# Splitting the weights of k ahead, in the first FFN, and keeping them in DRAM

## The chip, the cores and the metric

The kernel runs on one core of one Trainium2 chip. The metric is the device time of one execution in microseconds (us); the number given for a kernel is the median over runs. The profile is of one further execution. Engines: TensorE (PE; PEld is its weight load), VectorE (DVE), ScalarE (ACT), GpSimd (POOL) and SyncE (SP), which only issues transfers here. "PEq", "SPq" and so on are the engines' queues.

## The reference

A decoder trunk of two layers on `x` of 512 tokens by 1024 channels, all in float32: a gated linear recurrence (LRU) and a feed-forward network (FFN), then a time mixing (RWKV-7) and a second FFN, each behind an RMS norm and added to `x`; one more RMS norm at the end. What matters here is the first FFN and the first projections of the mixing:

```
# FFN, twice: 1024 -> 2 x 3072 -> 1024
u    = rmsnorm(x) @ w_up
gate = causal_conv3(u[:, :3072]) + conv_b
x    = x + (gelu(gate) * u[:, 3072:]) @ w_down
# time mixing
h    = rmsnorm(x);  xx = shift(h) - h
r, k, v = ((h + xx * mix[i]) @ w_rkv[i] for i in (0, 1, 2))
w, a, g = small two-step projections of h + xx * mix[3], mix[4], mix[5]
... per head: scan over the tokens with r, k, v, w, a; group norm; times g; @ w_out
```

## The kernel before

**Matmuls in three passes.** TensorE multiplies in a 32-bit format that rounds (`F32R`). To keep float32 accuracy each operand is split in two parts, hi = round(x) and lo = round(x - hi), and each product is made of three matmuls, hi.hi, hi.lo and lo.hi (`mm3`). Activations stand as channels by tokens, 128 x 512.

**Weights.** `plan_weights` lists all weights in the order of their use as pieces of 512 KB (128 partitions x 1024 numbers). For each piece, `weights_load` gets a raw tile and a transfer on SyncE's queue (line 166); `weights_split` (line 172) makes hi by a copy on ScalarE (line 94) and lo by a subtraction on VectorE (line 97). `next_weights` (line 188) hands out the next piece; it loads three pieces ahead and splits two ahead. Raw, hi and lo tiles, as many other tiles, come from one set of 21 slots of 4 KB per partition, `b4`; a transfer or an operation that wants a slot waits until one is released. The matmuls of one piece are 24 of 512 columns.

**The first FFN.** The 3072 hidden channels are done as 12 pairs of blocks of 128. Pairs 0, 1, 2, 4, 6, 8 and 10 are "whole": four pieces G0, U0, G1, U1 (gate and up, each for half of the 1024 input channels). Pairs 3, 5, 7, 9 and 11 are "halves": they save a part of the matmuls by combining weight halves, partly with accumulating transfers on GpSimd's queue (lines 168 and 748), in products 1, 5, 6, 2, 7, 4, 3. After a halves pair comes a part of the down projection, whose first piece's matmuls stand before its products 4 and 3. One round, a whole pair, a halves pair and four pieces of down, takes 64 us. The gate's evacuation writes a padded tile `gpad`, the convolution and GELU make `ge` from it (`gate`, line 682), and the up part is multiplied by `ge`. Pair n uses `gpads[n % 2]`; `ge` has two buffers.

**The stage behind it.** The last down projection makes `x` block by block, and with it the next norm's squares. `rwkv_lora` multiplies the small projections, `rwkv_lora_k` starts k (its eight pieces in two groups of four; `project(mk, ...)`) together with the second step of the small projections; the second group of k stands at the start of `rwkv_krv`, beside `prepare`, which turns k, w and a into the scan's operands. Then come r (eight pieces), v, and the scan by chunks. The norm's root is computed on GpSimd (line 334), as are some constant tiles at the start of `rwkv_krv` (lines 1133 to 1141).

**Order.** A scheduler orders the instructions of each engine before the run, by their order in the program and its own estimate of when each can start; at run time every engine works through its queue in that order. Work at the side is written as generators in three lanes; `background(n, lane)` advances a lane by n steps, fractions adding up.

Of the kernel before, what the change touches and what calls it, by code (L numbers as in the profile page):

```python
# [7 lines left out]
F32 = mybir.dt.float32  # L8
F32R = mybir.dt.float32r
# [4 lines left out]
DRAM = bass.MemoryType.DRAM  # L14
NOSYNC = mybir.DependencyInfo(mybir.DependencyClass.NoSync, mybir.DependencyReason.DATA)

P = 128
D = 1024
T = 512
# [8 lines left out]
N4 = 21  # L28
WARM2 = 20
WARM = 14  # L30

HALVES = (3, 5, 7, 9, 11)

# [11 lines left out]
class Kernel:  # L45
# [54 lines left out]
    def plan_weights(self):  # L100
        I = self.I
        plan = []
        self.quads = []

        def piece(w, r0, c0, k):
            return w[r0 : r0 + k * P, c0 : c0 + D // k].rearrange("(k p) c -> p k c", p=P)

        def add(w, r0, c0, k=2):
            plan.append((piece(w, r0, c0, k), k, False, None))

        def full(w, groups, rows=8):
            for g in groups:
                for k in range(0, rows, 2):
                    add(w, k * P, g * 512)

        def ffn(l):
            up, dn = I["ffn_w_up"][l], I["ffn_w_down"][l]

            def gu(six):


                for n in range(2 * six, 2 * six + 2):
                    self.quads.append(len(plan))
                    a = lambda i, j: piece(up, j * 512, (1 - i) * DFF + n * 256, 4)
                    if n in HALVES:
                        for first, more in (((0, 0), None), ((1, 1), (1, 0)), ((0, 1), None), ((1, 0), (0, 0)), ((1, 1), None)):
                            plan.append((a(*first), 4, True, more and a(*more)))
                    else:
                        for i, j in ((1, 0), (0, 0), (1, 1), (0, 1)):
                            plan.append((a(i, j), 4, False, None))  # L130
                self.quads.append(len(plan))

            def dd(row, n):
                for g in range(2):
                    for k in range(0, n, 2):
                        add(dn, row + k * P, g * 512)

            gu(0)
            for six in range(1, 6):
                gu(six)  # L140
                if six < 5:
                    dd((six - 1) * 512, 4)
            dd(2048, 8)

        full(I["lru_w_in"][0], [2, 3, 0, 1])
        full(I["lru_w_out"][0], [0, 1])
        ffn(0)
        for i in (1, 0):
            full(I["rwkv_w_rkv"][0, i], [0, 1])
        for g in range(4):  # L150
            for k in range(0, 8, 4):
                add(I["rwkv_w_rkv"][0, 2], k * P, g * 256, 4)
        for h in range(2):
            for g in range(4):
                add(I["rwkv_w_out"][0], h * 512, g * 256, 4)
        ffn(1)
        self.plan = plan
        self.loaded, self.splitted = {}, {}
        self.n_load = self.n_split = self.n_used = 0

    def weights_load(self, upto):
        while self.n_load < min(upto, len(self.plan)):
            i = self.n_load
            src, k, _, more = self.plan[i]
            raw = self.b4(F32, (k, D // k), f"raw{i}")
            self.nc.sync.dma_start(raw, src)
            if more is not None:
                self.nc.gpsimd.dma_start(raw, more, accum_op=ALU.add)  # L168
            self.loaded[i] = raw
            self.n_load += 1  # L170

    def weights_split(self, upto, pin=False):
        while self.n_split < min(upto, len(self.plan)):
            i = self.n_split
            if self.plan[i][2]:
                self.n_split += 1
                continue
            self.weights_load(i + 1)
            raw = self.loaded.pop(i)
            k = self.plan[i][1]  # L180
            hi = self.b4(F32R, (k, D // k), f"wh{i}")
            lo = self.b4(F32R, (k, D // k), f"wl{i}")
            for j in range(k) if i == 0 else [slice(0, k)]:
                self.split(raw[:, j], hi[:, j], lo[:, j], pin=pin)
            self.splitted[i] = (hi, lo)
            self.n_split += 1
# [46 lines left out]
    def setup(self):  # L233
        self.tasks, self.due, self.done = ([], [], []), [0, 0, 0], set()
        nc, tc, ctx = self.nc, self.tc, self.ctx
        self.const = ctx.enter_context(tc.tile_pool(name="const", bufs=1))
        self.psum = ctx.enter_context(tc.tile_pool(name="psum", bufs=1, space=PSUM))
        self.xsp = ctx.enter_context(tc.tile_pool(name="xsp", bufs=1))
        dram = ctx.enter_context(tc.tile_pool(name="dram", bufs=1, space=DRAM))
        self.xd = dram.tile([P, KB, T], F32, name="xd")  # L240
        self.tgd = dram.tile([160, T], F32, name="tgd")
        c = self.const
        self.x = c.tile([P, KB, T], F32, tag="x", name="x", bufs=1)
        self.ident = c.tile([P, P], F32, name="ident")
        make_identity(nc, self.ident)
        self.inv_d = c.tile([P, 1], F32, name="inv_d")
        nc.vector.memset(self.inv_d, 1.0 / D)
        self.mhalf = c.tile([P, 1], F32, name="mhalf")
        nc.scalar.mul(self.mhalf, self.inv_d, -0.5 * D)
        self.pv = c.tile([P, 4 * P], F32, name="pv")  # L250
        self.col = {}
        for g, group in enumerate(PARAMS):
            r = 0
            for name, n in group:
                self.col[name] = g * P + r
                r += n
# [329 lines left out]
    def ffn(self, l, xs, finish, after=None):  # L586
        nc, tc = self.nc, self.tc
        last = l == 1
        with tc.tile_pool(name=f"ffn{l}", bufs=1) as pool:
# [1 line left out]
                return pool.tile([P, n], dt, tag=tag, name=tag, bufs=bufs)  # L591

            rbs, norm = [], []
            gpads = [pool.tile([P, 2, T + 2], F32, name=f"gpad{i}") for i in range(2)]
            for u in gpads:
                nc.vector.memset(u[:, :, 0:2], 0.0)
            late = []
# [78 lines left out]
            class Pair:  # L676

                def __init__(pair, n):
                    pair.n, pair.gp = n, gpads[n % 2]
                    pair.w, pair.bank, pair.s = {}, {}, {}  # L680

                def gate(pair, e):
                    if not e:
                        pair.ge = pool.tile([P, 2, T], F32, tag="ge", name="ge", bufs=2)
                    fb = 2 * pair.n + e
                    cv = t("cv", 2)
                    cw = lambda j: self.vec(f"ffn_conv_w{l}", j * FB + fb)
                    nc.scalar.activation(cv, pair.gp[:, e, 0:T], AF.Identity, bias=self.vec(f"ffn_conv_b{l}", fb), scale=cw(0))  # L688
                    for j in range(1, 3):
                        nc.vector.scalar_tensor_tensor(cv, pair.gp[:, e, j : j + T], cw(j), cv, ALU.mult, ALU.add)  # L690
                    nc.scalar.activation(pair.ge[:, e], cv, AF.Gelu_apprx_tanh)
# [5 lines left out]
            class Whole(Pair):  # L697
# [5 lines left out]
                def product(pair, p):  # L703
                    hi, lo = self.next_weights()
                    k0 = int(p[1]) * 4
                    for e in range(2):
                        if not k0:
                            pair.bank[p[0], e] = self.bank("acc" + p[0])
                        ps = pair.bank[p[0], e]
                        for k in range(4):  # L710
                            c = slice(e * P, e * P + P)
                            self.mm3(ps, (hi[:, k, c], lo[:, k, c]), xs[k0 + k][:2], k0 + k == 0, k0 + k == 7)
                        if p == "G1":
                            tt(pair.gp[:, e, 2:], ps, rbs[0], ALU.mult)
                            pair.gate(e)
                        if p == "U1":
                            if not e:
                                pair.room()
                            un = t("s", 7)
                            tt(un, ps, pair.ge[:, e] if last else rbs[0], ALU.mult)  # L720
                            if not last:
                                tt(un, un, pair.ge[:, e], ALU.mult)
                            self.split(un, pair.hid[:, e, 0], pair.hid[:, e, 1])
                        self.background(1)

            class Halves(Pair):

# [149 lines left out]

            for n in range(3, 12, 2):
                products((n, 7))
                if n == 11 and not last:  # L880
                    self.norm_begin()
                    self.push(self.lora_weights())
                down(n, 2 * n - 6, 4 if n < 11 else 8, lambda: products((n, 3)), lambda: ahead(at[0] + 2))
# [897 lines left out]
```

## Time and profile before

| | |
|---|---|
| median of 3 runs | 1290.84 us (1290.55 to 1292.97) |
| profiled execution | 1291.05 us, of it 1289.3 from the first to the last instruction (the span) |
| TensorE busy | 1264.2 us (98%) |
| VectorE busy | 928.1 us (72%) |
| ScalarE busy | 642.8 us (50%) |
| GpSimd busy | 133.6 us (10%) |
| moved by DMA | 141.37 MB, mean 110 GB/s |

Busy times are the engines' own; matmuls are pipelined, so a busy TensorE is not one at its peak. [...] "Idle before ... <- releaser" in a row is the time in which an engine stood still before that instruction, and what it waited for last.

### The profile page before, as it was taken

What the parts mean: (1) busy time and instruction counts of PE and PEld (TensorE: products, weight loads), DVE (VectorE), ACT (ScalarE), POOL (GpSimd) and SP (SyncE); (2) the same over time, 40 slices, a digit from 0 to 9 for tenths busy, and PEclk for the clock granted to TensorE, in tenths of its full rate; (3) what the DMA queues carried; (4) which work ended last, traced back from release to release, by engine and by line L of the source; (5) the groups of instructions that cost most, each with busy time, mean ns of one, the idle gap of its engine ahead of it and who ended that gap; (6) DMA issues with size and microseconds to landing.
All of it is one profiled execution on the core that took longest, in us unless ns stands there. A gap on an engine that the chain in (4) does not pass through costs nothing. (4 is left out here: it accounts for less than half of the span.)

```text
span 1289.3 us, 22401 instructions
## 1 busy us (share of the span) xinstructions
PE 1264.2 (98%) x9259; PEld 1067.0 (83%) x9259; DVE 928.1 (72%) x1412; ACT 642.8 (50%) x1006; POOL 133.6 (10%) x206
## 2 busy tenths in 40 slices
PE   9999999999999999999899999999999999999998
PEld 8777888989898888877678888778889898988886
DVE  5998678757575766788999967778766566666653
ACT  6797455434343443559844346545644334343432
POOL 3000001010101010010002145410010101010100
PEclk9999999999999999999999999999999999999999
DMA  7312335455454544422212122132344454545431
GB/s 222 111 55 94 98 122 108 150 112 159 103 164 98 170 95 116 144 79 82 79 41 87 52 62 84 44 99 82 116 96 161 101 170 92 178 84 179 100 131 65
DMA packets 117829, 141.37 MB, mean 110 GB/s; under 512 B 10138, under 2 KB 91748, under 8 KB 117600
## 3 DMA queue, kind: packets, MB, share of 16 engines
q1 hardware_dynamic: 100528, 122.44, 29.8%
q0 software_dynamic: 16624, 16.47, 8.4%
q8 instruction: 72, 1.18, 0.4%
q10 hardware_dynamic: 576, 1.05, 0.2%
q14 instruction: 29, 0.24, 0.1%
HBM read 135.41 MB, written 4.52 MB: 109 GB/s over the span
## 5 line engine op out<-in xcount | busy, mean ns | idle before, releaser
L97 DVE TENSOR_TENSOR wl<-raw,wh 128x1024 fp32r<-128x1024 f32 (+1 forms) x161 | 194.4, 1213 | 124.7 <-ACT wh L94 104.0
L94 ACT CAST wh<-raw 128x1024 fp32r<-128x1024 f32 (+1 forms) x161 | 165.9, 1043 | 195.2 <-PE acc L54 56.0
L54 PE MATMUL accG<-xs,wh 128*128 128x512 f32 x448 | 138.7, 391 | 0.0
L54 PE MATMUL accU<-xs,wh 128*128 128x512 f32 x448 | 138.6, 391 | 0.0
L54 PE MATMUL acc<-hid,wh 128*128 128x512 f32 x384 | 119.8, 395 | 0.0
L744 DVE TENSOR_TENSOR lo<-raw,hi 128x1024 fp32r<-128x1024 f32 x70 | 85.5, 1222 | 39.4 <-PE accU L54 32.0
L743 ACT CAST hi<-raw 128x1024 fp32r<-128x1024 f32 x70 | 73.6, 1052 | 60.7 <-PE accU L54 25.3
L54 PEld LDWEIGHTS accG<-xs,wh 128*128 128x128 f32 x448 | 83.7, 188 | 17.3
L54 PEld LDWEIGHTS accU<-xs,wh 128*128 128x128 f32 x448 | 83.7, 188 | 17.2
L54 PE MATMUL accG<-xs,wl 128*128 128x512 f32 x224 | 87.3, 390 | 0.0
L54 PE MATMUL accU<-xs,wl 128*128 128x512 f32 x224 | 87.3, 390 | 0.0
L54 PEld LDWEIGHTS acc<-hid,wh 128*128 128x128 f32 x384 | 71.3, 187 | 16.7
L54 PE MATMUL accA<-xt,hi 128*128 128x256 f32 x480 | 83.4, 277 | 0.0
L54 PE MATMUL acc<-xs,wh 128*128 128x512 f32 x256 | 81.1, 398 | 0.0
L690 DVE SCALAR_TENSOR_TENSOR cv<-gpad,pv,cv 128x512 f32<-128x512 f32 x96 | 69.1, 748 | 12.3 <-ACT cv L688 11.8
L845 PE MATMUL acc<-wl,hid 128*128 128x512 f32 (+1 forms) x200 | 77.2, 386 | 0.0
L844 PE MATMUL acc<-wh,hid 128*128 128x512 f32 (+1 forms) x200 | 77.0, 385 | 0.0
L843 PE MATMUL acc<-wh,hid 128*128 128x512 f32 (+1 forms) x200 | 76.7, 383 | 0.0
L168 POOL DMA_DIRECT2D raw<-in_ffn_w_up_dram x20 | 25.7, 1285 | 480.8 <-DMA raw<-in_ffn_w_up_dram 336.3
L54 PE MATMUL acc<-hid,wl 128*128 128x512 f32 x192 | 75.0, 395 | 0.0
L54 PEld LDWEIGHTS accA<-xt,hi 128*128 128x128 f32 x480 | 73.2, 188 | 0.9
L54 PE MATMUL accA<-xt,lo 128*128 128x256 f32 x240 | 66.3, 276 | 0.0
(411 smaller groups left out, 2943.1 us busy)
## 6 DMA issues: line engine op xcount, KB each, us to landing
raw<-in_ffn_w_up_dram SPq DMA_DIRECT2D x106, 512.0 KB, 3.7
raw<-in_ffn_w_down_dram SPq DMA_DIRECT2D x48, 512.0 KB, 3.9
raw<-in_ffn_w_up_dram POOLq DMA_DIRECT2D x30, 512.0 KB, 5.9
raw<-in_rwkv_w_rkv_dram SPq DMA_DIRECT2D x24, 512.0 KB, 3.7
raw<-in_lru_w_in_dram SPq DMA_DIRECT2D x16, 512.0 KB, 4.3
raw<-in_lru_w_out_dram SPq DMA_DIRECT2D x8, 512.0 KB, 3.7
raw<-in_rwkv_w_out_dram SPq DMA_DIRECT2D x8, 512.0 KB, 3.6
xd<-x SPq DMA_DIRECT2D x8, 256.0 KB, 2.0
```

The source lines that it names most:

```text
L54: mm = lambda *a, **kw: self.nc.tensor.matmul(ps, *a, skip_group_check=more, **kw)
L94: put = (self.nc.vector.tensor_copy if dve else self.nc.scalar.copy)(hi, src)
L97: self.nc.vector.tensor_tensor(lo, src, hi.bitcast(F32), ALU.subtract)
L168: self.nc.gpsimd.dma_start(raw, more, accum_op=ALU.add)
L690: nc.vector.scalar_tensor_tensor(cv, pair.gp[:, e, j : j + T], cw(j), cv, ALU.mult, ALU.add)
L743: nc.scalar.copy(hi, f[p])
L744: tt(lo, f[p], hi.bitcast(F32), ALU.subtract)
L843: nc.tensor.matmul(ps, hh[:, s], wh[:, k, m], start=kk == 0, stop=False)
L844: nc.tensor.matmul(ps, hl[:, s], wh[:, k, m], start=False, stop=False)
L845: nc.tensor.matmul(ps, hh[:, s], wl[:, k, m], start=False, stop=kk == blocks - 1)
```

## The change

The eight pieces of k's weights (`AHEAD = 8`) are split during the first FFN. A generator, `split_ahead`, is pushed to lane 1 after product 7 of pair 3. Each of its ten steps loads a raw piece on GpSimd's queue into a tile `early` of the FFN's pool (two buffers), stores the hi and lo parts of the piece split in the step before to DRAM, also on GpSimd's queue, and splits the piece loaded in the step before. Whole pairs advance it by 0.32 twice a product; what is left is done before the last down projection. When `weights_load` comes to one of these pieces it gets two `b4` tiles and fetches the stored hi and lo on GpSimd's queue; `weights_split` passes them through. The first FFN now has one `gpad` and one `ge` buffer in place of two each (the second FFN keeps two).

```diff
@@ -29,6 +29,8 @@
 WARM2 = 20
 WARM = 14
 
+AHEAD = 8
+
 HALVES = (3, 5, 7, 9, 11)
 
 PARAMS = [
@@ -145,6 +147,7 @@
         full(I["lru_w_in"][0], [2, 3, 0, 1])
         full(I["lru_w_out"][0], [0, 1])
         ffn(0)
+        self.ahead = range(len(plan), len(plan) + AHEAD)
         for i in (1, 0):
             full(I["rwkv_w_rkv"][0, i], [0, 1])
         for g in range(4):
@@ -155,19 +158,46 @@
                 add(I["rwkv_w_out"][0], h * 512, g * 256, 4)
         ffn(1)
         self.plan = plan
-        self.loaded, self.splitted = {}, {}
+        self.loaded, self.splitted, self.stored = {}, {}, {}
         self.n_load = self.n_split = self.n_used = 0
 
     def weights_load(self, upto):
         while self.n_load < min(upto, len(self.plan)):
             i = self.n_load
             src, k, _, more = self.plan[i]
+            if i in self.stored:
+                self.loaded[i] = tuple(self.b4(F32R, (k, D // k), f"{part}{i}") for part in ("wh", "wl"))
+                for t, d in zip(self.loaded[i], self.stored[i]):
+                    self.nc.gpsimd.dma_start(t, d)
+                self.n_load += 1
+                continue
             raw = self.b4(F32, (k, D // k), f"raw{i}")
             self.nc.sync.dma_start(raw, src)
             if more is not None:
                 self.nc.gpsimd.dma_start(raw, more, accum_op=ALU.add)
             self.loaded[i] = raw
             self.n_load += 1
+
+    def split_ahead(self, pool):
+
+        raws, parts = {}, {}
+        n = self.ahead.stop
+
+        for i in range(self.ahead.start, n + 2):
+            if i < n:
+                src, k = self.plan[i][:2]
+                raws[i] = pool.tile([P, k, D // k], F32, tag="early", name="early", bufs=2)
+                self.nc.gpsimd.dma_start(raws[i], src)
+            if i - 2 in parts:
+                k = self.plan[i - 2][1]
+                self.stored[i - 2] = [self.dram.tile([P, k, D // k], F32, name=f"{part}d{i - 2}") for part in ("wh", "wl")]
+                for t, d in zip(parts.pop(i - 2), self.stored[i - 2]):
+                    self.nc.gpsimd.dma_start(d, t.bitcast(F32))
+            if i - 1 in raws:
+                k = self.plan[i - 1][1]
+                parts[i - 1] = [self.b4(F32R, (k, D // k), f"{part}{i - 1}") for part in ("eh", "el")]
+                self.split(raws.pop(i - 1), *parts[i - 1])
+            yield 1
 
     def weights_split(self, upto, pin=False):
         while self.n_split < min(upto, len(self.plan)):
@@ -177,6 +207,10 @@
                 continue
             self.weights_load(i + 1)
             raw = self.loaded.pop(i)
+            if i in self.stored:
+                self.splitted[i] = raw
+                self.n_split += 1
+                continue
             k = self.plan[i][1]
             hi = self.b4(F32R, (k, D // k), f"wh{i}")
             lo = self.b4(F32R, (k, D // k), f"wl{i}")
@@ -236,7 +270,7 @@
         self.const = ctx.enter_context(tc.tile_pool(name="const", bufs=1))
         self.psum = ctx.enter_context(tc.tile_pool(name="psum", bufs=1, space=PSUM))
         self.xsp = ctx.enter_context(tc.tile_pool(name="xsp", bufs=1))
-        dram = ctx.enter_context(tc.tile_pool(name="dram", bufs=1, space=DRAM))
+        dram = self.dram = ctx.enter_context(tc.tile_pool(name="dram", bufs=1, space=DRAM))
         self.xd = dram.tile([P, KB, T], F32, name="xd")
         self.tgd = dram.tile([160, T], F32, name="tgd")
         c = self.const
@@ -591,7 +625,7 @@
                 return pool.tile([P, n], dt, tag=tag, name=tag, bufs=bufs)
 
             rbs, norm = [], []
-            gpads = [pool.tile([P, 2, T + 2], F32, name=f"gpad{i}") for i in range(2)]
+            gpads = [pool.tile([P, 2, T + 2], F32, name=f"gpad{i}") for i in range(1 + l)]
             for u in gpads:
                 nc.vector.memset(u[:, :, 0:2], 0.0)
             late = []
@@ -676,12 +710,12 @@
             class Pair:
 
                 def __init__(pair, n):
-                    pair.n, pair.gp = n, gpads[n % 2]
+                    pair.n, pair.gp = n, gpads[n % len(gpads)]
                     pair.w, pair.bank, pair.s = {}, {}, {}
 
                 def gate(pair, e):
                     if not e:
-                        pair.ge = pool.tile([P, 2, T], F32, tag="ge", name="ge", bufs=2)
+                        pair.ge = pool.tile([P, 2, T], F32, tag="ge", name="ge", bufs=1 + l)
                     fb = 2 * pair.n + e
                     cv = t("cv", 2)
                     cw = lambda j: self.vec(f"ffn_conv_w{l}", j * FB + fb)
@@ -722,6 +756,7 @@
                                 tt(un, un, pair.ge[:, e], ALU.mult)
                             self.split(un, pair.hid[:, e, 0], pair.hid[:, e, 1])
                         self.background(1)
+                        self.background(0.32, 1)
 
             class Halves(Pair):
 
@@ -877,7 +912,11 @@
 
             for n in range(3, 12, 2):
                 products((n, 7))
+                if n == 3 and not last:
+                    self.push(self.split_ahead(pool), 1)
                 if n == 11 and not last:
+                    while self.tasks[1]:
+                        self.background(1, 1)
                     self.norm_begin()
                     self.push(self.lora_weights())
                 down(n, 2 * n - 6, 4 if n < 11 else 8, lambda: products((n, 3)), lambda: ahead(at[0] + 2))
```

## Rows read from the trace of the kernel before

**Rows 1.** The page: busy time of the engines, share of the span, instructions.

```profile
PE 1264.2 (98%) x9259; PEld 1067.0 (83%) x9259; DVE 928.1 (72%) x1412; ACT 642.8 (50%) x1006; POOL 133.6 (10%) x206
```

**Rows 2.** Windows in the first FFN: stretch, length, engines, clock, DMA share, GB/s.

```profile
314.00:336.00 22.00, 22.00 (x96) 17.79 (x95) 13.97 (x20) 5.49 (x7) 2.53 (x2) 1.00 0.61 154
314.00:378.00 64.00, 64.00 (x363) 55.73 (x362) 41.91 (x53) 25.20 (x31) 3.81 (x3) 1.00 0.50 132
```

**Rows 3.** Waits of TensorE, 560 to 700 us: us in total, times, longest.

```profile
PE acc L54 <- ACT wh L94: 3.5, 2, 3.0
PE knb L1211 <- DVE rec L1205: 1.2, 1, 1.2
PE acc L54 <- DVE wl L97: 0.5, 1, 0.5
```

**Rows 4.** Timeline of ScalarE in k's stage: start, us, instruction.

```profile
604.50 1.28 ACT L1169 ACT_TABLE_LOAD   x1 [1.28 <-DMA tgd<-lf]
...
615.89 1.03 ACT L94 CAST wh<-raw 128x1024 fp32r<-128x1024 f32 x1
```

**Rows 5.** Timeline of TensorE around its longest wait there.

```profile
613.09 0.62 PE L54 MATMUL acc<-mix,wh 128*128 128x512 f32 x2
613.55 0.40 PE L54 MATMUL acc<-mix,wl 128*128 128x512 f32 x1
616.97 3.25 PE L54 MATMUL acc<-mix,wh 128*128 128x512 f32 x7 [3.02 <-ACT wh L94]
620.02 0.63 PE L54 MATMUL acc<-mix,wl 128*128 128x512 f32 x1
```

**Rows 6.** Windows in and behind k's stage, columns as in rows 2.

```profile
617.00:620.00 3.00, 3.00 (x7) 2.35 (x8) 3.00 (x5) 3.00 (x7) 0.00 (x0) 0.52 0.01 3
660.00:700.00 40.00, 40.00 (x328) 32.62 (x330) 39.54 (x88) 15.20 (x30) 5.22 (x16) 1.00 0.23 73
700.00:740.00 40.00, 36.95 (x752) 34.32 (x756) 36.10 (x78) 18.42 (x37) 9.37 (x14) 1.00 0.17 55
```

**Rows 7.** Groups by line, 568 to 624 us: ScalarE's copies, VectorE's subtractions.

```profile
L94 ACT CAST wh<-raw 128x1024 fp32r<-128x1024 f32 x8 | 8.4, 1044 | 0.0
...
L97 DVE TENSOR_TENSOR wl<-raw,wh 128x1024 fp32r<-128x1024 f32 x7 | 8.5, 1215 | 0.3 <-ACT wh L94 0.3
```

**Rows 8.** Timelines of ScalarE, VectorE, TensorE: one split in whole pair 6.

```profile
335.10 1.05 ACT L94 CAST wh<-raw 128x1024 fp32r<-128x1024 f32 x1 [4.18 <-PE accG L54]
...
336.19 1.22 DVE L97 TENSOR_TENSOR wl<-raw,wh 128x1024 fp32r<-128x1024 f32 x1 [2.28 <-ACT wh L94]
...
340.57 0.62 PE L54 MATMUL accG<-xs,wh 128*128 128x512 f32 x2
```

**Rows 9.** The page: DMA queues (packets, MB, share), and one group of issues.

```profile
q1 hardware_dynamic: 100528, 122.44, 29.8%
q0 software_dynamic: 16624, 16.47, 8.4%
...
raw<-in_ffn_w_up_dram POOLq DMA_DIRECT2D x30, 512.0 KB, 5.9
```

**Rows 10.** GpSimd: issues by line (ns min/median/max), landing of the 30, timeline.

```profile
L1724 POOL DMA_DIRECT2D fg<-in_final_norm_dram x1: 576/576/576, 1225.1 to 1225.1; - x1
...
L168 POOL DMA_DIRECT2D raw<-in_ffn_w_up_dram x8: 1258/1267/1275, 260.7 to 459.7; - x8
...
DMA to landing us min/median/max: 5.7/5.9/9.1
...
550.32 1.03 POOL L334 TENSOR_TENSOR rs<-ms,mhalf 128x4 f32<-128x4 f32 x1 [77.78 <-DVE ms L328]
...
604.55 0.23 POOL L1133 MEMSET sel<- 128x160 f32 x1 [26.79 <-DMA tgd<-lf]
```

**Rows 11.** Timeline of VectorE at the start of the first FFN: `ge`, `gpad`.

```profile
206.47 0.69 DVE L722 TENSOR_TENSOR s<-s,ge 128x512 f32<-128x512 f32 x1
...
216.09 0.69 DVE L714 TENSOR_TENSOR gpad<-accG,rb 128x512 f32<-128x512 f32 x1 [0.32 <-PE accG L54]
```

## The prediction

> **What bounds the kernel now.** I read the page first: TensorE is busy for 98% of the span [rows 1], so a change to VectorE, ScalarE or the queues can only win where TensorE stands still or runs slowly. The second view is the list of TensorE's waits, stage by stage. In the first FFN it has no entry at all, and a whole round of its work, 64 us, shows TensorE busy for 64.00 [rows 2]. The stage of the change's weights, 560 to 700 us, has 5.2 us in the three rows that matter, and most of it is one wait for a ScalarE copy of line 94, 3.0 us [rows 3].
>
> The third view, the timeline, says which weights those are. k has eight pieces, whose copies on ScalarE can be counted through; k6's, the seventh, begins only at 615.89 [rows 4]. TensorE issued its last product of k5 at 613.55 and then stood still until k6's copy was done, 616.97 [rows 5]. It restarted slowly: the seven products from 616.97 to 620.02 took 3.05 us, where two before the gap took 0.46 (613.09 to 613.55), 0.23 each. [...] So this gap costs 3.02 us and then 3.05 - 7 x 0.23 = 1.44 us: 4.46 us. ScalarE was late because it had waited for a small store, `tgd<-lf`, until 604.50, loaded a table and had then done its other work of the stage before k6's copy [rows 4].
>
> Behind it, from 660 to 700 us, VectorE is busy 39.5 of 40 us beside a full TensorE [rows 6]: what reaches this stretch early is only worth something if VectorE is ahead as well.
>
> **What the change removes.** All eight splits of k leave the stage. Between 568 and 624 us that is seven subtractions on VectorE, 8.5 us, and seven of the eight copies that stand there on ScalarE (the eighth is r's first), 7 x 1.044 = 7.3 us [rows 7]. TensorE no longer waits for k6: 4.46 us. The splits of r, which stay, are the next to be late: 0.5 us for a copy (the second wait of that row, 3.5 - 3.0) and 0.5 for a subtraction [rows 3]; by then the two engines have 7 to 8 us less behind them, so I count this 1.0 us as gained, at most that and at least nothing. The 1.2 us of `knb` for `rec` [rows 3] hang on a chain of small steps rather than on the engines' load; I count nothing of it, and 1.2 as its bound. Sum: 4.46 + 1.0 = 5.5 us. VectorE must also be at least that much ahead at 660, and 8.5 us is more.
>
> **What it adds in the first FFN.** `split_ahead` makes ten steps, at 0.64 a product, so 2.56 in each whole pair 4, 6, 8 and 10. A step has one load, one split and two stores. The splits add 2.56 x (1.05 + 1.22) us per whole pair; with VectorE at 14 and ScalarE at 5.5 of 22 us [rows 2] they go into idle time. If that cover is gone, one split stands 2.3 us ahead of the next one that TensorE needs. That one has a lead: the copy at 335.10 is followed by its subtraction, done at 337.41, and the products of its piece begin at 340.57, of which the third is the first to need it, so at 341.0 [rows 8]: 3.6 us are left. I take nothing.
>
> DMA: the hardware queue moves 512 KB in 0.298 x 1289.3 / (122.44 / 0.524) = 1.64 us of all 16 engines, the software queue (GpSimd's, nearly all accumulating) in 0.084 x 1289.3 / (16.47 / 0.524) = 3.45 us [rows 9]. These are the bounds for the new transfers, since no plain transfer of this shape on GpSimd's queue is in the trace. Per round of whole pair, half pair and down projection (64 us) 7.7 transfers add 12.6 to 26.5 us, and the engines are now busy 0.50 x 64 = 32 us of it [rows 2]. That is 45 to 59 of 64: room, and the loads' own lead hides it. Nothing counted; nearer the low end, as the new transfers don't accumulate.
>
> GpSimd pays 0.58 us (the broadcast of line 1724) to 1.27 us (an accumulating transfer) for each issue [rows 10]: 24 issues in the FFN, where it works under 2.6 us in 22. That is free unless the accumulating transfers of the half pairs queue behind a store that waits; a stall there would show as TensorE waiting for the half pair's `hi` or `lo`, and it has no such wait now.
>
> The halved buffers: `ge` is last read for pair 1 at 206.47 to 207.16, and pair 2's gate is evacuated into `gpad` from 216.09 [rows 11]; `gpad`'s readers come earlier still. A lead of 8.9 us at the tightest of the places that I found, where three whole pairs follow each other. Nothing.
>
> **What it adds in k's stage.** Sixteen fetches of 512 KB on GpSimd's queue, two per piece: 3.3 to 6.9 us of the 16 engines against 24 x 0.23 = 5.5 us of products per piece. k0 to k2 can be fetched before 560; five pieces remain and have 572 to 613. Landing takes 5.9 us after issue on that queue [rows 9]. On GpSimd they are queued with the `rs` of the norm (550.32), and with the memsets from 604.55, which wait for that same `tgd<-lf` [rows 10]. A piece held 3 slots of the 21 of `b4` while it was split and now holds 2 from its fetch on. With the fetch two to three pieces ahead, 11 to 16 us against 2 x 1.27 + 5.9 = 8.4: hidden, but not by much.
>
> So 1291.05 (the profiled run, 1289.3 of it span) - 5.5 = 1285.5; that run is 0.2 us above the median of the three, 1290.84, and I predict 1285.3.
>
> **Rivals.**
> *Late fetches.* If the fetches of k6 and k7 stand behind the memsets that begin at 604.55 (say 1 us of them), four issues at 1.27 us begin at 605.6, 606.8, 608.1 and 609.4, and 5.9 us later k6 has landed (612.7) and then k7 (615.3). TensorE wants k6 at 613.9 and k7 six products later, 615.3: nothing lost. At the longest landing of that queue, 9.1 us [rows 10], k6 comes at 615.9 and k7 at 618.5: 3.2 us lost and the slow clock's 1.4, 4.6 in all. Or two fetches get in front of `rs`, 2.5 us. Against it: without the splits the `lf` chain, and with it the memsets, come some us earlier. The result is 1285.3 + 2.5 to 1285.3 + 4.6, 1287.8 to 1289.9: mostly no change. [...]
>
> *Starved whole pairs (slower).* The new `eh` and `el` take two to four of the 21 slots of `b4` until their stores have landed, 2 x 1.27 + 5.9 = 8.4 us. The splits of a whole pair already wait for TensorE to release slots (4.18 us of idle ScalarE before the copy at 335.10 [rows 8]). If such a split has to wait for a store, its lead of 3.6 us becomes a stall of 4.8, and with the slow clock behind it 6.2. One stall undoes the gain; one in each of two pairs gives 1285.3 + 12.4 = 1297.7, in all four 1310. For it: the slots are full. Against it: in every round ScalarE and VectorE have idle time to come back from a late split (25 and 42 us busy of 64 [rows 2]), so the second split would not be late by as much. [...]
>
> *The whole relief arrives.* VectorE is 8.5 us lighter. If it was the limit from 660 on, TensorE's other waits go too: 1.2 us of `knb`, and 40 - 36.95 = 3.05 us idle from 700 to 740 [rows 6]. Then 5.5 + 4.25 = 9.75 us, 1281.1.
>
> **Chances.** Forecast (1283 to 1288.2): 0.42. Whole relief (1279 to 1283): 0.20. Late fetches or a new wait of the same size (1288.2 to 1293.4): 0.20. Starved pairs: 0.18. A difference under 0.2%, 2.6 us, can't be told from none here; so faster 0.62, same 0.20, slower 0.18. The range runs from 1280 to 1294, leaving out about 0.05 below and 0.15 above.
>
> **What would show it.** Right: no copy or subtraction of line 94 or 97 on k's pieces after 560 us, no gap in TensorE between k5 and k6, a granted clock of 1.00 there, and TensorE as full as now in the FFN. Wrong: waits of TensorE for `wh` or `wl` in the whole pairs; a wait for a DMA in k's stage; `rs` late; or the gap of k6 reappearing at r, when its splits are no earlier.

## The result, and the profile after

The changed kernel took 1297.99 us (median of 5 runs, 1296.73 to 1299.20) where the kernel before took 1290.84 in runs beside it: ratio 1.0047, interval 1.0032 to 1.0062. That is 6 us slower by the ratio, 7 by the medians. I had predicted 1285.3, in a range of 1280 to 1294.

In the new file the lines have moved: line 94 is now 96, 97 is 99, 743 and 744 are 778 and 779, 765 (ScalarE's copy `s`) is 800, 748 and 168 (accumulating loads) are 783 and 177. In `split_ahead` the early loads are line 190 and the stores 195.

First k's stage, for which the change was made: TensorE's waits, 560 to 700 us, against [rows 3], and windows of it, against [rows 6]. (The list also has the norm's `rbc`, 0.9 us, which in the kernel before stands just ahead of 560.)

```profile
PE rec L1241 <- DVE n L1237: 0.8, 1, 0.8
PE acc L56 <- DVE wl L99: 0.5, 1, 0.5
PE acc L56 <- ACT wh L96: 0.5, 1, 0.5
```

```profile
617.00:620.00 3.00, 3.00 (x15) 2.49 (x14) 3.00 (x7) 3.00 (x8) 0.00 (x0) 1.00 0.29 68
660.00:700.00 40.00, 40.00 (x264) 32.34 (x262) 39.78 (x84) 14.30 (x24) 4.83 (x15) 1.00 0.25 73
700.00:740.00 40.00, 37.70 (x740) 34.92 (x739) 36.20 (x79) 20.18 (x43) 9.79 (x15) 1.00 0.14 42
```

The 3.0 us for `wh` are gone, and the clock granted to TensorE, as a share of its full one, is 1.00 where it had been 0.52 [rows 6]. There is no wait for a DMA. The two waits of 0.5 us stayed. The loss lies in the first FFN, where TensorE now has a wait (it had none), with a slow clock behind it (0.59 from 428 to 432):

```profile
PE accA L56 <- ACT s L800: 5.8, 1, 5.8
```

```profile
421.00:428.00 7.00, 1.16 (x8) 0.96 (x7) 5.64 (x8) 3.35 (x6) 0.00 (x0) 0.75 0.86 219
428.00:432.00 4.00, 4.00 (x24) 4.00 (x23) 2.00 (x3) 0.86 (x1) 0.00 (x0) 0.59 0.01 2
```

For a ledger, take the start of each matmul after minus the start of the same matmul before (the n-th on each accumulator). Ahead of the FFN the changed kernel is 0.7 us early. From 225 to 575 us it loses 2.4 us in steps of some ns, without a wait (I call this the creep); at 421 to 432 it loses 8.0 (5.84 of standing still, the rest at the slow clock behind it); at 615 to 635 it wins 4.7; near 810 it loses 0.5. That is 2.4 + 8.0 - 4.7 + 0.5 - 0.7 = 5.5, and the spans differ by 1294.7 - 1289.3 = 5.4.

How the stall came about stands in the timelines of GpSimd, ScalarE, SyncE and TensorE of the changed kernel, pairs 8 and 9:

```profile
402.41 1.25 POOL L190 DMA_DIRECT2D early<-in_rwkv_w_rkv_dram  x1
403.14 1.09 POOL L195 DMA_DIRECT2D wld<-el  x1
```

```profile
405.89 1.05 ACT L96 CAST wh<-raw 128x1024 fp32r<-128x1024 f32 x1 [5.42 <-DMA whd<-eh]
...
412.64 1.05 ACT L96 CAST eh<-early 128x1024 fp32r<-128x1024 f32 x1 [4.74 <-DMA wld<-el]
...
425.87 1.04 ACT L778 CAST hi<-raw 128x1024 fp32r<-128x1024 f32 x1 [2.57 <-DMA raw<-in_ffn_w_up_dram]
426.82 0.58 ACT L800 COPY s<-accA 128x512 f32<-128x512 f32 x1
```

```profile
420.15 0.37 SPq L175 DMA_DIRECT2D raw<-in_ffn_w_up_dram  x1
```

```profile
427.45 0.80 PE L56 MATMUL accA<-xt,hi 128*128 128x256 f32 x2 [5.84 <-ACT s L800]
```

ScalarE waits twice for a slot that a store still holds; the second store was issued at 403.14, and the copy begins at 412.64, 9.5 us later. So ScalarE and VectorE come some 8 us late to the half pair's pieces. A slot comes free late, and SyncE loads the raw piece of product 4 at 420.15 (412.06 before). Its copy stands in ScalarE's order ahead of the copy `s`, for which product 6 waits. So what TensorE waited for was not a whole pair's piece: the delay came to a half pair's through the order of ScalarE's work and a slot that came free late.

### The profile page after: what moved, and what is told of

It reads as the page before. It is cut to its first block, busy times and chain, and to the rows that moved or that the text cites. A ratio compares the mean times of both kernels' runs of the same rounds, so it can differ in the third digit from the quotient of the medians.

```text
span 1294.7 us, 22505 instructions
## 1 busy us (share of the span) xinstructions
PE 1267.4 (98%) x9259; PEld 1070.7 (83%) x9259; DVE 928.9 (72%) x1411; ACT 642.6 (50%) x1006; POOL 156.8 (12%) x246
## 5 line engine op out<-in xcount | busy, mean ns | idle before, releaser
L99 DVE TENSOR_TENSOR wl<-raw,wh 128x1024 fp32r<-128x1024 f32 (+1 forms) x153 | 184.7, 1213 | 111.3 <-ACT wh L96 91.9
L96 ACT CAST wh<-raw 128x1024 fp32r<-128x1024 f32 (+1 forms) x153 | 157.4, 1042 | 193.1 <-PE acc L56 56.2
L56 PE MATMUL accA<-xt,hi 128*128 128x256 f32 x480 | 86.5, 282 | 5.8 <-ACT s L800 5.8
```

The costliest lines, as they stand in the source:

```text
L56: mm = lambda *a, **kw: self.nc.tensor.matmul(ps, *a, skip_group_check=more, **kw)
L96: put = (self.nc.vector.tensor_copy if dve else self.nc.scalar.copy)(hi, src)
L99: self.nc.vector.tensor_tensor(lo, src, hi.bitcast(F32), ALU.subtract)
```

## The experiments

All are compared with the kernel before, run on the same chip; that kernel's median is 1290.84 to 1293.35 us from chip to chip, so the ratios count. Unless said otherwise a diff is against the changed kernel; `...` in a diff marks edits that are left out.

### Which half of the change loses

**buffers_only**: the single gate buffers alone.

```diff
-AHEAD = 8
+AHEAD = 0
...
-                if n == 3 and not last:
-                    self.push(self.split_ahead(pool), 1)
```

> One gpad and one ge buffer in the first FFN, nothing split ahead, k as before. Slot theory (the b4 slots of eh and el, held until their stores have landed, make ScalarE wait and so the raw piece of pair 9's product 4 late): no wait longer than before in the FFN, 1290.8 us, within 0.2% of before. Rival, single buffers: the stall of 5.8 us in pair 9 with its slow clock (8.0 in all) is here too, about 1299.

Ratio 1.0011 (0.9998 to 1.0024). No wait is new, but the ledger has the same creep, 2.3 us between 225 and 575. The creep belongs to the buffers, not to the transfers.

**ffn_only**: splits and stores in the first FFN, k's stage as before.

```diff
-            if i in self.stored:
+            if False:
...
```

> All that the change does in the first FFN, stores included, but k's pieces are then loaded raw on SyncE's queue and split in k's stage as before. The FFN's part, both theories: 8.0 us for the stall in pair 9 and 2.2 us of slightly slower matmuls between 240 and 560 us, so 1290.8 + 10.2 = 1301.0, and the 3.0 us gap of k6 still there. If k's stage gains nothing by the fetches: the same time as the whole change, 1298.

Ratio 1.0084 (1.0065 to 1.0102): the FFN's loss without the gain.

```profile
PE accA L56 <- ACT s L800: 6.3, 2, 5.8
...
PE acc L56 <- ACT wh L96: 3.4, 2, 3.0
```

**fetch_only**: the kernel before, k fetched as two parts, nothing split ahead.

```diff
+            if i in self.ahead:
+                self.loaded[i] = tuple(self.b4(F32R, (k, D // k), f"{part}{i}") for part in ("wh", "wl"))
+                for t in self.loaded[i]:
+                    self.nc.gpsimd.dma_start(t, src)
...
```

> No splitting ahead, two buffers each as before; both parts of each k piece are fetched from the raw weights on GpSimd's queue (so k is computed from wrong weights, hi and lo being the same raw numbers). k's stage alone: the gap of 3.0 us and its slow clock go, 4.7 us as between the two traces, so 1286.1, and no wait in the FFN. If the whole relief arrives when nothing in the FFN is lost: 1281. If the fetches cost as much as they save: 1290.8.

Ratio 0.9962 (0.9946 to 0.9978), 4.9 us: the whole gain without the FFN's loss. Sixteen fetches on GpSimd's queue cost k's stage nothing: TensorE has no wait for a DMA there, and none above 0.7 us.

**k6_k7_only**: only the last two pieces go through DRAM.

```diff
-        self.ahead = range(len(plan), len(plan) + AHEAD)
+        self.ahead = range(len(plan) + 6, len(plan) + AHEAD)
```

> Only k6 and k7 are split ahead, stored and fetched; four steps in place of ten, so all in whole pairs 4 and 6 and none in pair 8, before pair 9. Slot theory: what hurts is a store that holds slots just where a half pair's raw piece is waited for, so the stall may be gone; k's stage keeps its 4.7 us since only k6 was waited for: 1286 to 1288. If the gain needs all eight pieces off the two engines: 1290 to 1293, with the gap moved to another piece.

Ratio 1.0022 (1.0012 to 1.0032). No stall in the FFN, but of the gain only 0.4 us is left: `wh` is no longer late, and others are.

```profile
PE knb L1250 <- DVE rec L1244: 2.1, 1, 2.1
PE ssq L1218 <- ACT sq L1209: 0.9, 1, 0.9
```

**k6_first**: the kernel before, k6's split put ahead of the next stage's preparation.

```diff
+        self.weights_split(self.n_used + 3)
         self.push(prepare(0))
```

> The kernel before with one line more: the splits of the next pieces of k's weights are put into the engines' order ahead of the preparation of the next stage, nothing goes through DRAM, and the first FFN is untouched. Theory 'the order of one copy is all that k's stage gains': the gap of 3.0 us at k6 and its clock are gone, about 4.5 us less, 1286 to 1287 where before is 1291. Rival 'the engines are full there' (as splitting only pieces 6 and 7 ahead gained 0.4 us): the wait moves to rec and sq, 1290 to 1292.

Ratio 0.9997 (0.9986 to 1.0008). The gap at k6 is gone, some 4.6 us won by 624 us, and 5.8 are lost again by 640:

```profile
PE knb L1211 <- DVE rec L1205: 2.6, 1, 2.6
```

The rival holds: the splits must leave the two engines, their order alone brings nothing.

### What makes the stall

**own_room**: the parts get tiles of their own instead of slots of `b4` (one `early`, one `eh`, lo written over `early`).

```diff
-                parts[i - 1] = [self.b4(F32R, (k, D // k), f"{part}{i - 1}") for part in ("eh", "el")]
...
+            raw = pool.tile([P, k, D // k], F32, tag="early", name="early", bufs=1)
...
+            hi = pool.tile([P, k, D // k], F32R, tag="eh", name="eh", bufs=1)
...
```

> All eight pieces split ahead, stored and fetched, but without b4 slots: one early and one eh tile in the FFN's pool, the lo part written over early. Slot theory: no stall in pair 9 and no ScalarE wait for a store in front of a copy of wh or hi; k's stage keeps its 4.7 us; the 2.3 us of slightly slower matmuls that the single buffers alone show stay: 0.9965 to 0.999 of before. Traffic theory (stores and loads delay each other on the shared DMA engines): as many bytes move, so a stall of some us in a half pair stays, 1.002 or more.

Ratio 1.0122 (1.0102 to 1.0142). The stall of pair 9 is gone, and two others come to 16.4 us with their slow clock: TensorE waits 3.5 us for a `wl` of whole pair 2 and 8.5 in half pair 3. The wait in pair 2, and then GpSimd's and ScalarE's timelines ahead of the longer one:

```profile
217.59 0.50 PE L56 MATMUL accG<-xs,wl 128*128 128x512 f32 x1 [3.51 <-DVE wl L99]
```

```profile
213.01 0.73 POOL L185 DMA_DIRECT2D early<-in_rwkv_w_rkv_dram  x1 [5.66 <-DMA wld<-early]
...
226.43 0.55 POOL L197 DMA_DIRECT2D wld<-early  x1 [7.30 <-DVE early L194]
228.90 1.31 POOL L783 DMA_DIRECT2D raw<-in_ffn_w_up_dram  x1 [1.92 <-DVE lo L779]
229.67 1.27 POOL L185 DMA_DIRECT2D early<-in_rwkv_w_rkv_dram  x1
```

```profile
237.66 1.04 ACT L193 CAST eh<-early 128x1024 fp32r<-128x1024 f32 x1 [4.58 <-DMA early<-in_rwkv_w_rkv_dram]
...
243.46 0.58 ACT L800 COPY s<-accA 128x512 f32<-128x512 f32 x1
```

Its splits also begin earlier, at the FFN's start, so the place is not comparable; the chain is. No slot of `b4` is involved: the early load at 229.67 comes after the store and the accumulating load on GpSimd's queue, lands 8 us later, and its copy holds up ScalarE. But the single `early` tile is itself held until a store has landed (the load at 213.01 waited 5.66 us for that), so this run takes `b4`'s slots out of the chain, not every buffer that a store holds. My theory that the slots of `b4` alone were the cause fell here. **own_room_padded**, the same with rows of 528 elements in `gpad`, stalls in the same place.

> Both mends, no b4 slots and the padded gpad. Slot and placement theory together: the gain of k's stage alone, 4.7 us, 0.9955 to 0.9975 of before. If either is wrong: 0.998 or more.

Ratio 1.0139 (1.0123 to 1.0156).

**store_other**: the parts' slots come free after the subtraction; the raw tile is stored twice in their place.

```diff
-                for t, d in zip(parts.pop(i - 2), self.stored[i - 2]):
-                    self.nc.gpsimd.dma_start(d, t.bitcast(F32))
+                parts.pop(i - 2)
+                for d in self.stored[i - 2]:
+                    self.nc.gpsimd.dma_start(d, kept.pop(0))
...
+                kept += [raws[i - 1]] * 2
```

> As the change, with as many bytes stored, but the stores read the raw early tile, so eh and el give their slots back after the subtraction (what is stored and fetched for k is raw weights, k is computed wrong). Slot theory: the 8.0 us at pair 9 go, 0.996 to 0.999 of before. Traffic theory: the raw piece of pair 9's product 4 is as late as in the change and the stall stays, 1.005.

Ratio 1.0038 (1.0020 to 1.0057). Two smaller stalls, 4.0 us together, in other half pairs; here SyncE's load itself is late. It was issued at 286.24, amid four stores of GpSimd (282.91 to 286.40), and landed 9 us later:

```profile
286.24 0.37 SPq L175 DMA_DIRECT2D raw<-in_ffn_w_up_dram  x1
```

```profile
295.23 1.04 ACT L780 CAST hi<-raw 128x1024 fp32r<-128x1024 f32 x1 [5.40 <-DMA raw<-in_ffn_w_up_dram]
```

**no_store**: split ahead, parts dropped, raw piece fetched twice.

```diff
...
-                for t, d in zip(parts.pop(i - 2), self.stored[i - 2]):
-                    self.nc.gpsimd.dma_start(d, t.bitcast(F32))
+                self.stored[i - 2] = parts.pop(i - 2)
```

> The change, with the eight pieces of k loaded and split in the first FFN as before, but the two parts are dropped at once: nothing is stored, and k's stage fetches the raw piece twice in place of the two parts (so k is computed from other numbers). Theory 'stores' (slots held until stores land, and the stores' transfers beside the half pairs' own): no stall of TensorE in the first FFN, the creep of 2.3 us and the gain of about 5 us in k's stage stay, so 1287 to 1289 against 1291 for the kernel before. Rival 'splits' (the eight copies and subtractions themselves, 1.05 and 1.23 us each in engines that run in order): a stall of accA for ScalarE's copy s of 3 to 8 us stays, so 1291 to 1297.

Ratio 0.9975 (0.9964 to 0.9986), no stall: the splits' own 2.3 us each are hidden, as I had counted.

**traffic_only**: loads and stores, no split.

```diff
...
-                self.split(raws.pop(i - 1), *parts[i - 1])
+                parts[i - 1] = raws.pop(i - 1)
```

> The change with the eight raw pieces of k loaded in the first FFN and each stored twice as it is, with no split there (k's stage then multiplies by the raw piece as both parts, so k is computed from other numbers). No slot of the ring is held, and ScalarE and VectorE have no work more. Theory 'transfers' (the stores and early loads, 3 transfers of 512 KB per piece, make the half pairs' own pieces land late, or stand ahead of them in GpSimd's queue): a stall of 3 to 8 us somewhere in a half pair stays, 1291 to 1297. Rival 'splits or slots': no stall, 1287 to 1289.

Ratio 1.0033 (1.0017 to 1.0050), a stall of 4.3 us in pair 3. VectorE had waited for an accumulating load that GpSimd issued at 207.55 between two stores:

```profile
214.39 1.22 DVE L772 TENSOR_TENSOR raw<-raw,raw 128x1024 f32<-128x1024 f32 x1 [7.23 <-DMA raw<-in_ffn_w_up_dram]
```

**stores_sync**: the stores on SyncE's queue.

```diff
-                    self.nc.gpsimd.dma_start(d, t.bitcast(F32))
+                    self.nc.sync.dma_start(d, t.bitcast(F32))
```

> The change with its sixteen stores issued by SyncE in place of GpSimd; nothing else differs. Theory 'GpSimd queue' (accumulating loads stand behind stores that wait for a split): the stall of 8.0 us goes or falls below 2, about 1289 to 1292. Theory 'slots and transfers': the slots are held as long, the stall stays, 1296 to 1298; more, 1298 to 1303, if SyncE's raw loads now stand behind a store that waits for VectorE's subtraction.

Ratio 0.9994 (0.9978 to 1.0009); no stall in the FFN. The stores' line in the changed kernel, and then here (issues, who waited, landing):

```profile
L195 POOL DMA_DIRECT2D wld<-el x8: 532/574/1090, 278.9 to 460.1; - x8
...
  ACT eh L96: 6.5, 2
  ACT wh L96: 5.4, 1
...
  ACT hi L778: 3.3, 1
...
DMA to landing us min/median/max: 2.9/5.2/9.8
```

```profile
L195 SPq DMA_DIRECT2D wld<-el x8: 319/330/497, 278.7 to 458.4; - x8
...
  ACT wh L96: 3.2, 1
  ACT hi L778: 1.8, 1
...
DMA to landing us min/median/max: 2.6/3.0/6.8
```

Same splits, slots and bytes, another queue: the stores land in 3.0 us (median) in place of 5.2, at most 6.8 in place of 9.8, and ScalarE's waits for them fall from 15.2 to 5.0 us. It is not free: SyncE's own loads of the first FFN (200 to 550 us) land in 4.3 us (median) in place of 3.8, at most 6.9 in place of 8.4. Why a store lands sooner when SyncE issues it, no run shows.

### What makes the creep

**buffers_padded**: buffers_only with rows of 528 elements in `gpad`, in both FFNs.

```diff
-            gpads = [pool.tile([P, 2, T + 2], F32, name=f"gpad{i}") for i in range(1 + l)]
+            gpads = [pool.tile([P, 2, T + 16], F32, name=f"gpad{i}")[:, :, 0 : T + 2] for i in range(1 + l)]
...
```

> One gpad and one ge buffer, nothing split ahead, as the run with single buffers alone, but each gpad row is 16 in place of 2 numbers longer than 512, so that the tiles behind it begin at a multiple of 64 bytes as before. Placement theory: products of the xt tiles start every 113 ns again (117 with single buffers alone) and the 2.3 us go, 1.000 of before. If single buffers slow TensorE by waiting: 117 ns and 2.3 us stay.

Ratio 1.0028 (1.0008 to 1.0048). The guess of 64 bytes was wrong, but the intervals moved: 120 ns for the sums, 227 for the hidden values. In the second FFN, whose sums moved as well, 113 ns became 119. **hid_moved**, **sync_placed** and **sync_placed_hid** were to settle it:

```diff
-                minus = pool.tile([P, 4], F32, name="minus")
+                minus = pool.tile([P, 12 - 8 * l], F32, name="minus")[:, 0:4]
```

```diff
-            gpads = [pool.tile([P, 2, T + 2], F32, name=f"gpad{i}") for i in range(1 + l)]
+            gpads = [pool.tile([P, 2, T + 4 - 2 * l], F32, name=f"gpad{i}") for i in range(1 + l)]
...
```

> The kernel before, in which one tile of 4 elements ahead of the first FFN's hidden values becomes 12 elements wide, so that the hidden values lie 32 bytes further on; nothing else changes, and no buffer is dropped. Theory 'placement of the tile that a matmul streams sets its interval': the hidden values stand as far from a multiple of 64 bytes as in the version with rows of 528 elements, so their matmuls come every 227 ns in place of 233; 576 of them by 6.5 ns is 3.7 us less, ratio 0.997, and the other matmuls stay at 113. Rival 'the single buffers or something else in that version did it': 233 stays, ratio 1.000.

> The change with its stores issued by SyncE and the single gate buffer's rows 516 elements wide in place of 514 in the first FFN, so that the tiles behind it stand 32 bytes past a multiple of 4096, as behind two buffers of 514. Theory 'stall and creep are the whole loss, and the creep is placement': matmul intervals of 113 and 233 ns as before, no creep, no stall, and k's stage gains 4.7 us: 1286 where before is 1291, ratio 0.9965. Rival 'the creep belongs to the single buffers': intervals stay 117 and 234, creep of 2.3 us, ratio 0.998 to 0.9995 as with the stores on SyncE alone.

> The version before this one with the hidden values 32 bytes further on as well. Theory 'placement': intervals of 113 and 227 ns, 3.7 us less than that version, 1282 to 1283 where before is 1291, ratio 0.9935. Rival: no gain over it.

Ratios 0.9995 (0.9984 to 1.0006), 0.9980 (0.9969 to 0.9991), 0.9975 (0.9965 to 0.9985); no interval moved. The edits had moved nothing that is streamed: in the built programs `xt` begins at 132288 behind a `gpad` of 4112 bytes and behind one of 4128, and `minus` lies behind the hidden values. They stand as a repeat of the kernel before and two of stores_sync, so that one is 0.2% faster than before. From here on I read the places out of the built programs.

**hid_shift** (the kernel before), **sync_back** (stores_sync) and **sync_both** (sync_back with hid_shift's edit):

```diff
             sums = [pool.tile([P, 2, 4, H], F32R, tag="xt", name="xt", bufs=4) for _ in range(4)]
+            minus = pool.tile([P, 16 + 16 * l], F32, name="minus")[:, 0:4]
...
```

```diff
-            gpads = [pool.tile([P, 2, T + 2], F32, name=f"gpad{i}") for i in range(1 + l)]
+            gpads = [pool.tile([P, 2, T + 8 - 6 * l], F32, name=f"gpad{i}") for i in range(1 + l)]
...
```

> The kernel before, in which a small tile (made 64 bytes wide) is put ahead of the first FFN's hidden values, which then stand 32 in place of 96 bytes past a multiple of 128; no buffer is dropped. Theory 'address': the matmuls that stream hidden values come every 227 ns in place of 233, 576 of them by 6 ns, 3.5 us less, ratio 0.9973; those that stream the sums stay at 113. Rival 'the single buffers, or what else runs': 233 stays, ratio 1.000.

> The change with its stores issued by SyncE, and the single gate buffer's rows 520 elements wide in the first FFN, so that sums and hidden values stand 96 bytes past a multiple of 128 as in the kernel before. Theory 'stall and creep are the whole loss, and the creep is the address': intervals of 113 and 233 ns, no creep, no stall, k's stage gains 4.7 us: about 1286 where before is 1291, ratio 0.9965. Rival 'the creep belongs to the single buffers': 117 and 234 stay, ratio 0.998 to 0.9995.

> The version with the stores on SyncE and rows of 520 elements, with the hidden values at 32 bytes past a multiple of 128 as well. Theory 'address': intervals of 113 and 227 ns, 3.5 us less than that version, about 1283 where before is 1291, ratio 0.9935 to 0.994. Rival: no gain over it.

Ratios 0.9982 (0.9966 to 0.9998), 0.9957 (0.9942 to 0.9972), 0.9932 (0.9916 to 0.9949): all three as the address theory said. Places are bytes past a multiple of 128; intervals are the median distance of neighbouring starts, first FFN, 230 to 545 us.

| kernel | sums `xt` at | 256 columns | hidden values at | 512 columns |
|---|---|---|---|---|
| before | 96 | 113 ns | 96 | 233 ns |
| after, buffers_only, stores_sync | 64 | 117 | 64 | 234 |
| buffers_padded | 32 | 120 | 32 | 227 |
| hid_shift | 96 | 113 to 114 | 32 | 227 |
| sync_back | 96 | 113 | 96 | 233 |
| sync_both | 96 | 113 to 114 | 32 | 227 |

In every one of them `xs` lies at 32, and streams in 120 ns (256 columns) and 227 (512). Which modulus counts stays open: 96, 64 and 32 past a multiple of 128 are in these programs also 224, 192 and 32 past one of 256, and two tiles of later stages of the kernel before, `BK` and the mixing's `early`, at 32 past a multiple of 128 but 160 past one of 256, come every 232 ns (512 columns), beside other work.

The rows behind the 256 columns, before and then after; 21 matmuls take 2.38 and 2.46 us:

```profile
293.36 0.39 PE L54 MATMUL accA<-xt,hi 128*128 128x256 f32 x2
...
295.74 0.39 PE L54 MATMUL accA<-xt,hi 128*128 128x256 f32 x2
```

```profile
293.19 0.40 PE L56 MATMUL accA<-xt,hi 128*128 128x256 f32 x2
...
295.65 0.40 PE L56 MATMUL accA<-xt,hi 128*128 128x256 f32 x2
```

The rows behind the last column, after and then hid_shift; three matmuls take 0.70 and 0.68 us:

```profile
262.91 0.63 PE L56 MATMUL acc<-hid,wh 128*128 128x512 f32 x2
263.38 0.40 PE L56 MATMUL acc<-hid,wl 128*128 128x512 f32 x1
263.61 0.63 PE L56 MATMUL acc<-hid,wh 128*128 128x512 f32 x2
```

```profile
262.28 0.62 PE L54 MATMUL acc<-hid,wh 128*128 128x512 f32 x2
262.73 0.39 PE L54 MATMUL acc<-hid,wl 128*128 128x512 f32 x1
262.96 0.62 PE L54 MATMUL acc<-hid,wh 128*128 128x512 f32 x2
```

The creep follows: 480 matmuls on the sums (five half pairs, four products of 24) by 4 ns and 576 on the hidden values by 1 ns are 2.5 us; 2.3 to 2.4 were lost. sync_back lets stall and creep go together and is faster than before by 5.6 us by the ratio, 4.2 by the medians and 2.5 between the two profiled spans; k's stage alone is worth 4.7, so what is left unnamed is some 2 us at most. sync_both, 1286.23 us beside 1293.26, is 7.0 us faster than before by the medians, 8.8 by the ratio: the version that beats both.

## Why the prediction was wrong

- **k's stage, 4.46 us: right.** 4.7 measured, by the steps given: the copy of k6 leaves, the gap and its slow clock go (1.44 us of the 4.46, at a clock of 0.52 [rows 6]).
- **The 1.0 us at r: not there.** Both waits of 0.5 us are as before [rows 3], with 7 to 8 us less work ahead of them. That they came from the engines' load was wrong. ScalarE's timelines, before and then after, show what stands ahead of r's copy:

```profile
646.38 0.65 ACT L1286 COPY D<-aab 128x256 f32<-128x256 f32 x2 [1.23 <-PE aab L1281]
...
650.08 2.94 ACT L94 CAST wh<-raw 128x1024 fp32r<-128x1024 f32 x3
```

```profile
651.20 0.65 ACT L1325 COPY D<-aab 128x256 f32<-128x256 f32 x2 [1.22 <-PE aab L1320]
...
654.89 2.94 ACT L96 CAST wh<-raw 128x1024 fp32r<-128x1024 f32 x3
```

ScalarE waits 1.2 us for TensorE's own product `aab`, makes ten small copies of it and only then r's copy. TensorE's pace sets its time here: with less work for ScalarE ahead of it that wait is 1.22 us in place of 1.23.
- **Late fetches: did not come.** No run has a wait of TensorE for a fetch; a plain transfer of GpSimd took 0.53 to 0.73 us to issue where nothing overlapped it, near my low bound of 0.58, not the 1.27 that this rival needed.
- **The whole relief: did not come.** VectorE is busy 39.78 of 40 us at 660 to 700 us, as in [rows 6], although seven subtractions left ahead of it: it was not the load before 660 that filled it. From 700 to 740 TensorE idles 2.3 us in place of 3.05. The 1.2 us of `knb` did go, but a new wait of 0.8 for `n` stands just ahead of it, at `rec`.
- **"Nothing" for splits, transfers and GpSimd's queue in the FFN: the step that failed, 8.0 us.** The splits were rightly free (no_store). I counted transfers by mean occupancy over 64 us, 45 to 59 of 64, and called that room. What counted was the landing of one store amid other transfers: up to 9.8 us, at the moment when a slot or a queue behind it was needed. I had named the place, accumulating transfers queued behind a store, and dismissed it because TensorE has no wait there now. That shows that the lead is long enough today, not how long it is.
- **The slower rival, 0.18, was the near one.** Its stall was worked out as 4.8 us, 6.2 with the clock, per starved pair; one of 5.84 came, 8.0 with the clock. The time for which a store holds a slot was near as well: 8.4 us worked out, 9.5 measured at the stall. But it was to strike whole pairs' splits, and in the changed kernel it struck a half pair's raw piece (a whole pair's `wl` is late in own_room, 3.5 us). So the rival had the size nearly right and the place wrong.
- **"Nothing" for the halved buffers: 2.3 us.** Their lead of 8.9 us was right, there is no new wait. I had not thought that dropping a tile would move those behind it, and that the matmuls' pace would change with their place (113 to 117 ns, 233 to 234).

Shown: the stall is due to the stores on GpSimd's queue. The kernels with them and all eight pieces have waits of TensorE of 4.0 to 12 us there; in the five with the stores on SyncE no wait of TensorE there is above 0.8; without stores there is no stall. Open: how much of it is the slots held, how much the accumulating and early loads behind or beside a store. own_room, store_other and traffic_only stall without the parts' slots (in all three a store holds the `early` tile instead), and in the changed kernel ScalarE waits for slots, so both take part; no run has them singly under the same timing.

## What to carry to other kernels

Where an engine's order is full of short leads, as here, look at a transfer's worst landing at the moment that somebody waits for what it holds, which was 9.5 us at the stall, and not only at the mean occupancy of the DMA engines, 45 to 59 of 64 us as I had worked it out. The queue that issues a store is worth a run of its own: here the same sixteen stores cost 8.0 us from GpSimd, amid its accumulating loads, and left no wait above 0.8 from SyncE, although SyncE's plain loads have deadlines too. Splits that left a full stage helped when all eight of them left (4.9 us in fetch_only, 0.4 with two pieces): moving one copy forward moved the wait by as much (4.6 us won, 5.8 lost). After an edit that drops or adds a tile, look at the distance between the starts of neighbouring matmuls (113 ns became 117 here) as well as at the waits.

## What the runs showed of the hardware

- In the first FFN the pace of the matmuls changed with the place of the tile that they stream. By bytes past a multiple of 128: with 256 columns 113 ns at 96 (before), 117 at 64 (after), 120 at 32 (buffers_padded); with 512 columns 233, 234 and 227 in the same three. So of the three places 32 was best for 512 columns and worst for 256. Why, no run tells; a place at 0 was not tried, and whether 128 is the modulus isn't shown.
- A store of 512 KB landed in 2.9 to 9.8 us (median 5.2) when issued by GpSimd (after), in 2.6 to 6.8 (median 3.0) when issued by SyncE (stores_sync), in the same stretch of the same work.
